# A streaming encoder step on one core: ScalarE's order written down, weights at fixed distances ahead, sums of squares in another bank, branch stages in half-range steps

## The chip, the cores and the metric

The kernel runs on one core of one Trainium2 chip. The metric is the device time of one launch in microseconds (us): 3112.74 us, the median of three runs (3103.7, 3112.74 and 3119.0). The engines are called as in the profile: PE (TensorE's matmuls; PEld is its weight loads), DVE (VectorE), ACT (ScalarE), POOL (GpSimd) and SP (SyncE, which issues most DMAs here).

## The reference, cut to what matters

One layer of a hybrid encoder over two requests that share weights: 2048 first frames of a new stream, and 64 frames of a running one. All data is fp32.

```
n = RMSNorm(h)
[z | xBC | dt | u | pool_gate | merge_logits] = n @ W_in            # 1024 x 10272
x, B, C = split(silu(causal_dwconv(xBC, 4 taps)))
per chunk of 64 frames, per group of 4 heads:                        # 8 groups
    L  = exp(acum[l] - acum[s]) for l >= s, else 0                   # acum = cumsum(dt * A)
    y  = (C B^T * L) @ (x dt) + (C @ state) * exp(acum)
    state = state * exp(acum[-1]) + B^T @ (x dt exp(acum[-1] - acum))
a = GatedGroupRMSNorm(y + D x, silu(z)) @ W_branch_ssd               # mean square over a group's 256 columns
b = (MultiScalePool(u) @ pool_w * silu(pool_gate)) @ W_branch_pool
h = h + (sigmoid(g_a) * a + sigmoid(g_b) * b) @ W_out;  y = RMSNorm(h)
```

Outputs are y of both requests and the carried states (SSD, convolution, pooling).

## The kernel before, in words

The 2112 frames are done in three parts of T = 704 frames, each in two halves of H = 352. Within a part, the columns of W_in come in pairs of 256 columns, and a `Pair` is computed by seven products instead of eight (a Strassen-like scheme, on sums of the blocks of W_in and on sums N[1..7] of the normalised input). Each weight block is split into a high and a low float32r piece (`split`: ACT writes the high one at L179, DVE the low one at L180), and each of the four k-steps takes three matmuls. So an *item* of PE's work is mostly one product of one pair: 12 matmuls of 352 columns.

`Stream` holds all items of all three parts in order, and *events* between them: functions that issue work of other engines, or a few matmuls, at a position counted in items. `prepare` fetches and splits weights for items ahead, as far as the eight weight slots are free. In `Pair.prep`, the step for product 1 loads both raw column blocks (`cols`, to a tile `wraw`), the step for product 6 has POOL compute three sums (L254 to L256), the step for product 5 a fourth (L260). The split blocks of the u, x and bc pairs are stored to memory in part 1 and loaded back in parts 2 and 3; z, gate and pool-gate pairs are split anew in each part. That makes 40 + 20 + 20 = 80 pairs with sums.

Within a product, results go through banks `a`, `d` and `e`; `keep` copies `a` to a tile e1, e2 or e3 on ACT (L282), and `store` (L290, L292) writes results out on ACT or adds them on DVE.

A part's phases are: u and pool-gate pairs; then for each of 8 groups its bc, x and z pairs, with the group's 6 SSD *units* (128 frames each, 48 units a part, 144 in all) placed in between as events; then gate pairs; then the pool branch, the SSD branch and the output product; and the norm of the next part.

A unit has four events. `unit_load` loads bA (the decay logarithms, L732, a DMA on ACT's queue) and POOL masks it (`affine_select`, L733). `unit_front` has ACT turn bA into exponentials (L749, four of them, one for each head) and PE transpose x and B (bank `tp`). `decay_load` loads eB. `unit_back` does PE's y product (bank `y`) and the new state's product (bank `st`); POOL scales the old state (L800), DVE reads y (L803, L804) and adds the new state to the scaled one (L805), which frees bank `st`.

After a group's last unit, `group_post` gates y; its square is taken on ACT (L817) and summed by two small matmuls with a column of ones (`group_rms`, tiles `sqr`, one call for each half, in bank `st`); in the last part `group_state` transposes both final states, one after the other, in bank `st`, and ACT copies each to a tile `ho` (L852).

PE runs its matmuls in program order (`mm` and `transpose` pin them). The order of ACT, DVE, POOL and of the DMA issues is chosen by the scheduler of the language, from what it assumes of durations, and is then fixed in the compiled program: each engine works through its list in order.

Of the kernel before, what the change touches and what calls it, by code (L numbers as in the profile page):

```python
# [8 lines left out]
F32 = mybir.dt.float32  # L9
# [7 lines left out]
P = 128  # L17
DM = 1024
KT = 8
# [47 lines left out]
class Stream:  # L67

    def __init__(self, slots):
        self.items, self.events = [], []
        self.slots, self.ready, self.out, self.n = slots, 0, 0, 0

    def add(self, prep, use, ns=1, free=None):
        self.items.append((ns, prep, use, [], ns if free is None else free))
        return len(self.items)
# [4 lines left out]
    def prepare(self, limit):  # L82
        while self.ready < len(self.items) and self.out + self.items[self.ready][0] <= limit:
            ns, prep, use, got, _ = self.items[self.ready]
            got.append(prep() if prep else None)
            self.out += ns
            self.ready += 1

    def run(self):
        ev = sorted(self.events, key=lambda e: e[:2])  # L90
        for i, (ns, prep, use, got, free) in enumerate(self.items):
            while ev and ev[0][0] <= i:
                ev.pop(0)[2]()
            self.prepare(self.slots)
            if use:
                use(got[0])
            self.out -= free
        for e in ev:
            e[2]()
# [3 lines left out]
def kernel(  # L103
# [24 lines left out]
    dma, dma_a = nc.sync.dma_start, nc.scalar.dma_start  # L128
    V, S, G = nc.vector, nc.scalar, nc.gpsimd
# [77 lines left out]
    def cunit(w, c0, r0=0):  # L207

        r = cols(w, c0, r0)
        out = []  # L210
        for i in range(2):
            s = split_slot(r[:, i * 512:(i + 1) * 512])
            out += [(s, k) for k in range(4)]
        return out
# [18 lines left out]
    class Pair:  # L233
# [6 lines left out]

        def prep(self, i):
            wd = wc_d.get(self.key)
            if wd is not None and not self.q.first:
                return load_slot(wd[:, i - 1])
            if i == 1:
                self.r0, self.r1 = [cols(w_in, c) for c in pair_cols[self.key]]
                self.a11, self.a12 = self.r0[:, 0:512], self.r0[:, 512:1024]
                self.a21, self.a22 = self.r1[:, 0:512], self.r1[:, 512:1024]
                src = self.a11
            elif i == 2:  # L250
                src = self.a12
            elif i == 6:
                self.s3 = s_tile()
                G.tensor_tensor(out=self.s3, in0=self.a11, in1=self.a21, op=ALU.subtract)  # L254
                G.tensor_tensor(out=self.a21, in0=self.a21, in1=self.a22, op=ALU.add)
                G.tensor_tensor(out=self.a11, in0=self.a21, in1=self.a11, op=ALU.subtract)  # L256
                src = self.a11
            elif i == 5:
                self.s4 = s_tile()
                G.tensor_tensor(out=self.s4, in0=self.a12, in1=self.a11, op=ALU.subtract)  # L260
                src = self.a21
            else:
                src = {7: lambda: self.s3, 4: lambda: self.a22, 3: lambda: self.s4}[i]()
            s = split_slot(src)
            if wd is not None:
                dma(wd[:, i - 1], flat_slot(s))
            return s
# [26 lines left out]
        def use(self, i, w):  # L294
# [26 lines left out]
            else:  # L321
                self.product(self.d, w, 3, False)
                self.store(self.d, 0, 1, self.e2)
                if self.tile_done:
                    self.tile_done(0)
                self.done()
# [22 lines left out]
    def row_scale(sp, ch, xt, junk):  # L349
# [5 lines left out]
        G.tensor_tensor(out=ss[0:L, 2:3], in0=ss[0:L, 1:2], in1=mhalf[0:L, 0:1], op=ALU.pow)  # L355
        S.activation(xt[0:L], xt[0:L], AF.Copy, scale=ss[0:L, 2:3])
# [64 lines left out]
    def begin():  # L421
# [9 lines left out]
        for ch in q.chunks:  # L431
# [4 lines left out]
            row_scale(n0, ch, xt, junk)  # L436
# [4 lines left out]
        stream.prepare(1)  # L441
# [10 lines left out]
        stream.prepare(2)  # L452
        s.factor(6)
        stream.prepare(3)
        s.factor(5)
        s.factor(7)
        stream.prepare(5)
# [21 lines left out]
        st.close()  # L479

    def add_part(qi, q):
# [39 lines left out]
        def dt_turn():  # L521
# [14 lines left out]
            V.scalar_tensor_tensor(out=ea, in0=dtf, scalar=-1.0, in1=dtf, op0=ALU.mult, op1=ALU.max)  # L536
            S.activation(ea, ea, AF.Exp, scale=-1.0)
# [10 lines left out]
            dtA = dts["A"] = tmp("dtA")  # L548
            V.tensor_tensor(out=dtA, in0=dt, in1=aneg.unsqueeze(1).broadcast_to([P, NC, 32]), op=ALU.mult)
            q.nacum, q.dtd, q.dec = stt("acum"), stt("dtd"), stt("dec")  # L550
            V.memset(q.dtd, 0.0)
            V.memset(q.nacum, 0.0)
# [36 lines left out]
        def u_pair(gi):  # L589
# [11 lines left out]
            def tile_done(jj):  # L601
# [19 lines left out]
                split(st["dhi"][:, jj], st["dlo"][:, jj], dd)  # L621
# [3 lines left out]
            return Pair(q, ("u", gi), open_, lambda: None, tile_done)  # L625

        def pg_pair(gi):
# [6 lines left out]
            return Pair(q, ("pg", gi), open_, lambda: S.activation(st["gs"], st["gs"], AF.Silu))  # L634

        def pool_prep(gi):
            praw = nm["pb"].tile([P, 512], F32, tag="praw", name="praw", bufs=1)
            dma(praw.rearrange("p (k c) -> p k c", c=256), pool_w[0, gi].rearrange("(k p) c -> p k c", p=P))
            return split_slot(praw)
# [29 lines left out]
        def conv_pair(g, name):  # L669
# [28 lines left out]
            return Pair(q, ("x" if name == "xx" else "bc", g), open_, done, tile_done)  # L698
# [491 lines left out]
```

## Time and profile before

| | |
|---|---|
| runs | 3103.7, 3112.74, 3119.0 us |
| profiled execution: its own time | 3116.79 us |
| its span | 3115.1 us |
| mean granted TensorE clock, of full speed | 0.972 |
| PE busy | 2903.4 us (93%), 18794 instructions |
| DVE busy | 1983.6 us (64%) |
| ACT busy | 1533.1 us (49%) |
| POOL busy | 849.0 us (27%) |

The span is cut into three parts of about 1000 us; the first has a start-up of some 50 us, and behind the last matmul stands a tail of 11 us. Stretches of the first part: u and pool-gate pairs until about 290 us, groups until 800, gate pairs until 850, branches and output until 1034; the second and third repeat this with stored weights. In the rows below a bracket behind an instruction says how long its engine had been idle before it, and what it waited for last.

### The profile page before, as it was taken

Reading aid. Unit: us, or ns where it says so; the run is one execution under the profiler, and the core shown is the slowest. Engines: PE = TensorE matmul, PEld = TensorE weight load, DVE = VectorE, ACT = ScalarE, POOL = GpSimd, SP = SyncE. Lnnn points to the kernel's source line nnn. Section 1 sums busy time; section 2 is a strip of 40 time slices with the busy share of each in tenths; the row PEclk is TensorE's granted clock in tenths of the full one; section 3 lists DMA queues with packets and bytes.
Section 4 is the critical chain, followed back from the end, with each engine's and each line's share of the span. In section 5 each row is a group of like instructions: output and inputs, shape, how many; then the busy total and the mean of one; then the engine's idle time right before and its main releaser. Section 6 shows DMA issues by size and latency. Waiting matters only on the chain. (4 is left out here: it accounts for less than half of the span.)

```text
span 3115.1 us, 50768 instructions
## 1 busy us (share of the span) xinstructions
PE 2903.4 (93%) x18794; PEld 2772.7 (89%) x18794; DVE 1983.6 (64%) x3444; ACT 1533.1 (49%) x2920; POOL 849.0 (27%) x996
## 2 busy tenths in 40 slices
PE   6989888989999999999999999999999999989998
PEld 6888888878899999989898899999999888879998
DVE  7767787887654566457667765365666666666532
ACT  5445566666443433356655653244355565555311
POOL 4344454445100022123323410012233233341000
PEclk8999999999999999999999999999999999999999
DMA  5565676774586664757576467465567756646743
GB/s 184 177 204 182 213 212 179 233 214 113 173 286 209 242 187 142 233 173 194 171 225 189 100 218 222 134 200 177 185 194 200 204 163 210 170 102 213 223 126 138
DMA packets 502796, 585.09 MB, mean 188 GB/s; under 512 B 43429, under 2 KB 400637, under 8 KB 502549
## 3 DMA queue, kind: packets, MB, share of 16 engines
q1 hardware_dynamic: 391189, 531.50, 52.9%
q10 hardware_dynamic: 111360, 50.36, 8.5%
q8 instruction: 148, 2.42, 0.3%
q14 instruction: 99, 0.81, 0.1%
HBM read 434.31 MB, written 147.44 MB: 187 GB/s over the span
## 5 line engine op out<-in xcount | busy, mean ns | idle before, releaser
L132 PE MATMUL ps_a<-N,w 128*128 128x352 f32 x5760 | 1022.0, 330 | 45.1 <-ACT e L282 42.3
L132 PEld LDWEIGHTS ps_a<-N,w 128*128 128x128 f32 x5760 | 946.6, 191 | 65.4 <-ACT e L282 51.3
L180 DVE TENSOR_TENSOR w<-wraw,w 128x512 fp32r<-128x512 f32 x560 | 462.6, 839 | 285.2 <-ACT w L179 276.7
L132 PE MATMUL ps_d<-N,w 128*128 128x352 f32 x2880 | 508.0, 332 | 4.3 <-DVE sa L292 3.0
L132 PEld LDWEIGHTS ps_d<-N,w 128*128 128x128 f32 x2880 | 477.5, 194 | 7.7 <-DVE sa L292 3.8
L179 ACT CAST w<-wraw 128x512 fp32r<-128x512 f32 x560 | 337.7, 618 | 253.8 <-POOL wraw L256 50.2
L749 ACT ACTIVATE bA<-bA,acum 128x128 f32<-128x128 f32 (+1 forms) x576 | 192.5, 385 | 259.0 <-POOL bA L733 250.4
L282 ACT COPY e<-ps_a 128x352 f32<-128x352 f32 x360 | 160.4, 446 | 303.4 <-PE ps_a L132 225.6
L132 PE MATMUL ps_e<-N,w 128*128 128x352 f32 x1440 | 265.1, 335 | 18.8 <-DVE zt L292 11.8
L132 PEld LDWEIGHTS ps_e<-N,w 128*128 128x128 f32 x1440 | 242.1, 196 | 22.6 <-DVE zt L292 13.0
L733 POOL TENSOR_SCALAR_AFFINE_SELECT bA<-bA 128x512 f32<-128x512 f32 x144 | 99.3, 689 | 426.7 <-DMA bA<-ac_d 404.3
L254 POOL TENSOR_TENSOR S<-wraw 128x512 f32<-128x512 f32 x80 | 125.0, 1563 | 214.9 <-DMA wraw<-in_w_in_dram 82.9
L689 DVE SCALAR_TENSOR_TENSOR xx<-raw,cwT,xx 128x704 f32<-128x704 f32 (+1 forms) x144 | 151.2, 1050 | 24.8 <-ACT xx L686 24.1
L800 POOL TENSOR_TENSOR h<-h,dec 128x256 f32<-128x256 f32 x136 | 101.6, 747 | 199.3 <-PE ps_y L132 196.9
L689 DVE SCALAR_TENSOR_TENSOR bc<-raw,cwT,bc 128x704 f32<-128x704 f32 (+1 forms) x144 | 139.3, 967 | 17.5 <-ACT bc L686 17.0
L260 POOL TENSOR_TENSOR S<-wraw 128x512 f32<-128x512 f32 x80 | 111.1, 1389 | 144.1 <-DVE w L180 132.4
L355 POOL TENSOR_TENSOR ss<-ss,mhalf 128x1 f32<-128x1 f32 (+1 forms) x18 | 11.0, 612 | 486.9 <-DVE ss L353 437.8
L132 PE MATMUL ps_a<-yn,w 128*128 128x352 f32 x798 | 131.3, 322 | 1.0 <-ACT w L179 0.8
L180 DVE TENSOR_TENSOR w<-S,w 128x512 fp32r<-128x512 f32 x160 | 114.5, 716 | 26.9 <-ACT w L179 26.9
L132 PE MATMUL ps_d<-yn,w 128*128 128x352 f32 x798 | 130.4, 322 | 0.0
L132 PEld LDWEIGHTS ps_a<-yn,w 128*128 128x128 f32 x798 | 128.0, 188 | 1.9 <-ACT w L179 1.1
L256 POOL TENSOR_TENSOR wraw<-wraw 128x512 f32<-128x512 f32 x80 | 117.5, 1468 | 41.6 <-DVE w L180 34.3
(292 smaller groups left out, 4976.2 us busy)
## 6 DMA issues: line engine op xcount, KB each, us to landing
wraw<-in_w_in_dram SPq DMA_DIRECT2D x160, 512.0 KB
w<-wc_x SPq DMA_DIRECT2D x112, 512.0 KB
w<-wc_bc SPq DMA_DIRECT2D x112, 512.0 KB
bA<-ac_d ACTq DMA_DIRECT2D x120, 256.0 KB
wc_x<-w SPq DMA_DIRECT2D x56, 512.0 KB
wc_bc<-w SPq DMA_DIRECT2D x56, 512.0 KB
w<-wc_u SPq DMA_DIRECT2D x56, 512.0 KB
wraw<-in_w_branch_ssd_dram SPq DMA_DIRECT2D x48, 512.0 KB
```

The lines of the kernel that those rows point to most:

```text
L132: tc.keep_in_program_order(nc.tensor.matmul(*a, **k))
L179: S.copy(out=dst_hi, in_=src)
L180: V.tensor_tensor(out=dst_lo, in0=src, in1=dst_hi.bitcast(F32), op=ALU.subtract)
L254: G.tensor_tensor(out=self.s3, in0=self.a11, in1=self.a21, op=ALU.subtract)
L256: G.tensor_tensor(out=self.a11, in0=self.a21, in1=self.a11, op=ALU.subtract)
L260: G.tensor_tensor(out=self.s4, in0=self.a12, in1=self.a11, op=ALU.subtract)
L282: S.copy(out=e, in_=ps[:, 0:H])
L355: G.tensor_tensor(out=ss[0:L, 2:3], in0=ss[0:L, 1:2], in1=mhalf[0:L, 0:1], op=ALU.pow)
L689: V.scalar_tensor_tensor(out=xx[:, i, 0:XL], in0=raw[:, t:t + XL], scalar=cwT[:, t, ct:ct + 1], in1=xx[:, i, 0:XL], op0=ALU.mult, op1=ALU.add)
L733: G.affine_select(out=bA[0:L, :, 0:L], in_=bA[0:L, :, 0:L], compare_op=ALU.is_ge, fill=-1e30, base=0, pattern=[[0, HPG], [1, L]], channel_ ...
L749: S.activation(bA[0:L, r, 0:L], bA[0:L, r, 0:L], AF.Exp, bias=q.nacum[0:L, ci, 4 * g + r:4 * g + r + 1])
L800: G.tensor_tensor(out=hd(hcur), in0=hd(hcur), in1=q.dec[:, ci, 4 * g:4 * g + 4].unsqueeze(2).broadcast_to([P, HPG, 64]), op=ALU.mult)
```

## The change

It has six pieces.

- **ACT's order is pinned.** From the end of `begin` on, copies, activations and DMA issues on ACT's queue are kept in the order of the program's text (class `S`, `dma_a`). So are POOL's weight sums (`pool_sum`) and its masks, the latter one item after bA's load was issued. DVE's order is still chosen by the scheduler.
- **Fixed distances.** An item's split is issued 5 items before its use and a stored block's load 7 before, where slots are free. The first raw load of a pair is issued 9 items before its product 1, the second 10 before product 6, three sums 7 before product 6, the fourth 12 before product 3. Some ACT work behind a product (Silu of z, x, bc and pool gate, splits of the pooled tile, softplus of dt) is issued some items later (`stream.later`).
- **Sums of squares in bank `y`.** `group_rms` moves from bank `st` to `y`, and stands behind the first `unit_front` that comes at least 4.4 items after `group_post`.
- **The final states** are transposed by two events, 1.5 items apart, and not behind each other.
- **Branch stages in half-range steps.** `pool_branch` and `ssd_branch` become two items each (one for each half of 352 frames, 24 or 48 matmuls), `out_product` one item for each block of 128 frames; gates, y and m0 are loaded and turned earlier, W_out's split happens in the pool branch's phase, and the next part's norm is spread over the output product, three items for each block of frames.
- **The last scaling** of an output block is done in 2 pieces of 512 columns instead of 4 of 256.

The work is nearly the same: PE has the same matmuls, ACT 147 table loads for 153.

PE's list at the end of the first group of part 1, before (bank `st` holds the new state of the group's last unit, the next unit's and then the squares' sum; `d`, `e` and `a` are products):

```order
L132 MATMUL ps_y_3313<-bA_3029,xdt_3116 64x128 x4
L132 MATMUL ps_y_3313<-bc_2850,h_3027 128x128 x2
L132 MATMUL ps_st_3320<-xdtd_3117,bt_3118 128x256
L132 MATMUL ps_d_3151<-N_149,w_3128 128x352 x12
L132 MATMUL ps_st_3347<-sqr_3206,onesr_111 32x352 x2
L132 MATMUL ps_d_3360<-N_151,w_3147 128x352 x12
```

and in the changed kernel:

```order
L183 MATMUL ps_y_3305<-bA_3022,xdt_3109 64x128 x4
L183 MATMUL ps_y_3305<-bc_2844,h_3020 128x128 x2
L183 MATMUL ps_st_3312<-xdtd_3110,bt_3111 128x256
L183 MATMUL ps_d_3143<-N_149,w_3157 128x352 x12
L183 MATMUL ps_d_3345<-N_151,w_3198 128x352 x12
L183 MATMUL ps_a_3204<-N_153,w_3219 128x352 x12
L186 MATMUL ps_tp_3385<-ident_81,xx_2624 128x128 x2
L186 MATMUL ps_tp_3385<-ident_81,bc_2844 128x128
L183 MATMUL ps_tp_3385<-bc_2844 128x128
L183 MATMUL ps_y_3399<-sqr_3279,onesr_111 32x352 x2
```

Between the matmul that writes a new state to `st` and the squares' sum stood one product; now three products and a unit's transposes stand there, and the sum is in bank `y`.

ACT's list at the first units of part 1, before (`e1` to `e3` are the copies that free bank `a`, `w` the high halves of weights, `bA` a unit's exponentials):

```order
L732 DMA bA_2406<-ac_d_126 128x4x128
L732 DMA bA_2486<-ac_d_126 128x4x128
L749 ACT_TABLE_LOAD
L749 ACTIVATE bA_2406<-bA_2406,acum_778 128x128
L179 CAST w_2051<-wraw_1951 128x512
L749 ACTIVATE bA_2406<-bA_2406,acum_778 128x128 x2
L179 CAST w_2068<-S_2009 128x512
L749 ACTIVATE bA_2406<-bA_2406,acum_778 128x128
L749 ACTIVATE bA_2486<-bA_2486,acum_778 128x128 x4
L282 COPY e3_2084<-ps_a_1957 128x352
```

and in the changed kernel:

```order
L177 DMA bA_2398<-ac_d_126 128x4x128
L170 CAST w_2400<-S_2296 128x512
L170 CAST w_2423<-wraw_2339 128x512
L170 COPY sa_2267<-ps_a_2235 128x11x32
L170 CAST w_2440<-wraw_2339 128x512
L170 COPY e2_2460<-ps_a_2380 128x352
L174 ACT_TABLE_LOAD
L174 ACTIVATE bA_2398<-bA_2398,acum_755 128x128 x4
L170 COPY bt_2473<-ps_tp_2466 128x128
L177 DMA bA_2478<-ac_d_126 128x4x128
```

The exponentials of two units, the second of them loaded just before, stood ahead of the copy `e3`; now a unit's exponentials stand together, behind the copies of the products before it, and the next unit's load is issued behind them.

The diff, cut to its core:

```diff
+    def later(self, k, fn):
+        self.pending.append((self.cur + k, fn))
+    def prepare(self, upto=None):
+        while self.ready < len(self.items):
+            ns, prep, use, got, free, lead = self.items[self.ready]
+            if self.ready - lead > self.cur or self.out + ns > self.slots:
+                return
...
+    class S:
+        @staticmethod
+        def pin(ins):
+            if fixed[0]:
+                tc.keep_in_program_order(ins)
+        @staticmethod
+        def copy(**k):
+            S.pin(nc.scalar.copy(**k))
...
+    def pool_sum(**k):
+        tc.keep_in_program_order(G.tensor_tensor(**k))
...
+            return {1: ((9, 1, self.load0),), 6: ((10, 1, self.load1), (7, 0, self.sums)),
+                    3: ((12, 0, self.sum4),)}.get(i, ())
...
-            if i == 1:
-                self.r0, self.r1 = [cols(w_in, c) for c in pair_cols[self.key]]
...
             dma_a(bA[0:L, :, 0:L], ac_d[4 * g:4 * g + 4, lt:lt + L].unsqueeze(0).broadcast_to([L, HPG, L]))
-            G.affine_select(out=bA[0:L, :, 0:L], in_=bA[0:L, :, 0:L], compare_op=ALU.is_ge, fill=-1e30, base=0,
+            stream.later(1, lambda: tc.keep_in_program_order(
+                G.affine_select(out=bA[0:L, :, 0:L], in_=bA[0:L, :, 0:L], compare_op=ALU.is_ge, fill=-1e30, base=0,
...
         def group_rms(g, h):
-            ps = tpsum("st")
+            ps = tpsum("y")
...
+            after[n, i] = stream.add(lambda pr=pr, i=i: pr.prep(i), lambda w, pr=pr, i=i: pr.use(i, w),
+                                     lead=7 if pr.stored() else 5, early=pr.early(i))
...
-                p = max(mid, ready("z", g)) + 0.01
+                p = max(mid, ready("z", g) + 1.5) + 0.01
+                after_f = [t for t in slots[u + 1:u + 1 + NC] if t >= p + 4.4] if g + 1 < NG else [p + 5, p + 8]
+                r0 = after_f[0]
+                r1 = [t for t in after_f if t >= r0 + 2][0]
                 stream.at(p, lambda g=g: group_post(g))
-                stream.at(p + 0.01, lambda g=g: group_sum(g, 0))
-                stream.at(p + 5, lambda g=g: group_rms(g, 0))
-                stream.at(p + 6, lambda g=g: group_state(g))
+                stream.at(p + 2, lambda g=g: group_square(g))
+                stream.at(p + 3.2, lambda g=g: group_sum(g, 0))
+                stream.at(r0 + 0.02, lambda g=g: group_rms(g, 0))
+                if q.last:
+                    stream.at(r0 + 0.03, lambda g=g: group_state(g, grp[g]["h"], ssd_p))
+                    stream.at(r0 + 1.5, lambda g=g: group_state(g, grp[g]["hs"], ssd_s))
...
-            stream.add(lambda j=j: cunit(w_bp, j * P), lambda u, j=j: pool_branch(j, u), 2)
+            stream.add(lambda j=j: column_blocks([got[0, j]]), lambda u, j=j: pool_branch(j, 0, u), 2, 0, 2,
+                       early=((4, 1, lambda j=j: get((0, j), w_bp, j * P)),))
+            stream.add(None, lambda u, j=j: pool_branch(j, 1, u), 0, 2)
```

## Rows read from the trace of the kernel before

**Rows 1.** Busy time by stretch: length, busy us (instructions) of each engine, clock.
```profile
core 0: us, PE busy (x) PEld busy (x) DVE busy (x) ACT busy (x) POOL busy (x), PEclk, DMA share, GB/s
50.00:290.00 240.00, 219.37 (x1328) 212.40 (x1329) 175.81 (x266) 110.26 (x203) 101.03 (x88) 0.96 0.61 200
290.00:800.00 510.00, 448.41 (x2883) 413.49 (x2882) 404.94 (x655) 320.08 (x612) 238.54 (x243) 0.95 0.62 184
850.00:1034.00 184.00, 183.25 (x1163) 181.87 (x1161) 93.86 (x148) 67.96 (x106) 1.01 (x2) 1.00 0.79 262
...
2300.00:2800.00 500.00, 463.32 (x3028) 431.27 (x3027) 334.27 (x627) 285.66 (x574) 172.24 (x253) 0.97 0.62 174
...
50.00:3104.00 3054.00, 2876.51 (x18670) 2749.60 (x18670) 1941.77 (x3351) 1500.35 (x2869) 830.90 (x972) 0.98 0.62 188
```

**Rows 2.** PE's waits, whole span: waiting for what: us, times, longest.
```profile
PE ps_st L132 <- DVE h L805: 50.7, 14, 8.4
PE ps_a L132 <- ACT e L282: 42.3, 27, 5.2
PE ps_st L135 <- ACT ho L852: 15.0, 8, 3.3
PE ps_e L132 <- DVE zt L292: 11.8, 3, 5.0
```

**Rows 3.** PE's waits in 290 to 800 us (the groups of part 1).
```profile
PE ps_st L132 <- DVE h L805: 34.0, 6, 8.4
PE ps_a L132 <- ACT e L282: 13.2, 11, 3.3
```

**Rows 4.** Timeline 405 to 428 us: start, duration, instruction, count, [idle before <- releaser].
```profile
417.43 1.29 POOL L254 TENSOR_TENSOR S<-wraw 128x512 f32<-128x512 f32 x1 [4.13 <-DMA wraw<-in_w_in_dram]
...
419.03 1.75 DVE L180 TENSOR_TENSOR w<-wraw,w 128x512 fp32r<-128x512 f32 x1
420.31 1.59 POOL L256 TENSOR_TENSOR wraw<-wraw 128x512 f32<-128x512 f32 x1
...
422.92 1.24 POOL L800 TENSOR_TENSOR h<-h,dec 128x256 f32<-128x256 f32 x1
...
424.83 0.41 DVE L804 TENSOR_TENSOR yt<-ps_y,yt 128x256 f32<-128x256 f32 x1
...
426.02 0.41 DVE L805 TENSOR_TENSOR h<-ps_st,h 128x256 f32<-128x256 f32 x1
...
426.58 0.77 PE L132 MATMUL ps_st<-sqr,onesr 128*32 128x352 f32 x2 [8.40 <-DVE h L805]
```

**Rows 5.** Timeline 219 to 231 us.
```profile
220.51 3.98 PE L132 MATMUL ps_d<-N,w 128*128 128x352 f32 x24
221.12 0.75 SPq L204 DMA_DIRECT2D wraw<-in_w_in_dram  x1
226.00 0.63 POOL L733 TENSOR_SCALAR_AFFINE_SELECT bA<-bA 128x512 f32<-128x512 f32 x1 [8.35 <-DMA bA<-ac_d]
226.67 1.28 ACT L749 ACTIVATE bA<-bA,acum 128x128 f32<-128x128 f32 x4 [7.89 <-POOL bA L733]
227.54 1.27 POOL L254 TENSOR_TENSOR S<-wraw 128x512 f32<-128x512 f32 x1 [0.90 <-DMA wraw<-in_w_in_dram]
...
229.21 0.43 ACT L282 COPY e<-ps_a 128x352 f32<-128x352 f32 x1
...
229.69 1.54 PE L132 MATMUL ps_a<-N,w 128*128 128x352 f32 x4 [5.20 <-ACT e L282]
```

**Rows 6.** Waits of all engines, whole span: us, times, longest.
```profile
POOL bA L733 <- DMA bA<-ac_d: 404.3, 97, 19.9
...
ACT bA L749 <- POOL bA L733: 250.4, 95, 8.3
```

**Rows 7.** DVE's groups by line, 850 to 1000 us: count, busy us, mean ns, idle.
```profile
L180 DVE TENSOR_TENSOR w<-wraw,w 128x512 fp32r<-128x512 f32 x51 | 33.4, 687 | 57.7 <-ACT w L179 57.5
```

**Rows 8.** The same in 300 to 800 us.
```profile
L180 DVE TENSOR_TENSOR w<-wraw,w 128x512 fp32r<-128x512 f32 x117 | 120.3, 1041 | 19.4 <-ACT w L179 19.2
```

More of the change, by code (lines that the diff above doesn't have):

```diff
@@ L87, in prepare, with first, soon @@
             self.ready += 1
-    def run(self):
[L90 to L94, printed above, removed]
+    def first(self):
+        self.pending = []
+        self.ev = sorted(self.events, key=lambda e: e[:2])
+        self.early.sort(key=lambda e: e[:3])
+    def soon(self, i):
+        while self.early and self.early[0][0] <= i:
+            self.early.pop(0)[3]()
+    def run(self):
+        for i, (ns, prep, use, got, free, lead) in enumerate(self.items):
+            self.cur = i
+            self.pending.sort(key=lambda e: e[0])
+            while self.pending and self.pending[0][0] <= i:
+                self.pending.pop(0)[1]()
+            while self.ev and self.ev[0][0] <= i:
+                self.ev.pop(0)[2]()
+            self.prepare()
+            self.soon(i)
             if use:
@@ L241, in prep @@
         def prep(self, i):
             wd = wc_d.get(self.key)
-            if wd is not None and not self.q.first:
+            if self.stored():
                 return load_slot(wd[:, i - 1])
-            if i == 1:
-                self.r0, self.r1 = [cols(w_in, c) for c in pair_cols[self.key]]
[L247 to L263, printed above, removed]
@@ L479, in begin @@
         st.close()
+        fixed[0] = True
     def add_part(qi, q):
@@ new lines, in y_load, with dense @@
+            ys.extend([(t, 0), (t, 1)])
+            return turn
+        def dense(ps, blocks, movs, off, ks, n):
+            for k in ks:
+                (s, c), (t, kk) = blocks[k], movs[k]
+                wh, wl = s[:, 0, c * P:(c + 1) * P], s[:, 1, c * P:(c + 1) * P]
+                a, b = t[:, 0, kk, off:off + H], t[:, 1, kk, off:off + H]
+                for i, (st_, mv) in enumerate(((wh, a), (wh, b), (wl, a))):
+                    mm(ps[:, 0:H], lhsT=st_, rhs=mv, start=k == 0 and i == 0, stop=k == n - 1 and i == 2)
@@ new lines, in add_part, with m0_load, ssd_branch, evict @@
+        m0s = {}
+        def m0_load(j):
+            m0s[j] = nm["py"].tile([P, T], F32, tag="rb", name="m0t", bufs=2)
+            dma(m0s[j], m0_d[j])
+        def ssd_branch(j, h, u):
+            u = held.setdefault(("s", j), u)
+            ga = gts[j]
+            def evict(ps, off):
+                V.tensor_tensor(out=ga[:, off:off + H], in0=ps[:, 0:H], in1=ga[:, off:off + H], op=ALU.mult)
+            if j == 0:
+                if h == 0:
+                    held["ps"] = [any_bank(), any_bank()]
+                    dense(held["ps"][0], u, ys, 0, range(14), 16)
+                else:
+                    dense(held["ps"][1], u, ys, H, range(14), 16)
+                    for i, off in enumerate((0, H)):
+                        dense(held["ps"][i], u, ys, off, range(14, 16), 16)
+                        evict(held["ps"][i], off)
+            else:
+                ps = any_bank()
+                dense(ps, u, ys, h * H, range(16), 16)
+                evict(ps, h * H)
+            if h:
+                V.tensor_tensor(out=ga, in0=ga, in1=m0s[j], op=ALU.add)
+                stream.later(1, lambda: split(nm["mhi"][:, j], nm["mlo"][:, j], ga))
@@ L1028, in add_part @@
         obase = len(stream.items)
         fin, hrow = [], {}
+        order = (NC - 1,) + tuple(range(NC - 1))
         def out_start():
+            close_pool("pt")
             close_pool("py")
```

417 lines of the change are left out of this document (244 added, 173 removed).

## The prediction

> **What bounds the kernel now.** I read the stretches first [rows 1]. From 50 to 3104 us PE is busy for 2876.51 of 3054 us; nothing else comes near that over the whole (DVE 1941.77, ACT 1500.35). Two quantities can be won while the matmuls stay the same: 3054 - 2876.5 = 177.5 us in which PE stands idle, and the clock. It was granted 0.98 of full speed on the mean, 0.02 x 3054 = 61 us lost. The reader is to see where: in 850 to 1034 us, the branches, PE is idle for 0.75 us and the clock is 1.00. Where PE is held up (290 to 800 us: 61.6 us idle; 2300 to 2800: 36.7) the clock is 0.95 and 0.97, which loses 25.5 and 15 us; 50 to 290 loses 9.6. Those three make 50 of the 61 us. So the loss of clock goes with the idle stretches, and I take it to shrink in proportion with them.
>
> Next, PE's waits [rows 2]: the first four are 50.7 us for a state addition ahead of the squares' sum, 42.3 for copies of bank a, 15.0 for the copy of a final state, 11.8 for an addition to z. They are spread thin behind that. The long ones are followed back in two pieces of the timeline.
>
> **The squares' sum.** In the worst case [rows 4] its matmul stood 8.40 us idle until 426.58. It needed bank st, which DVE's L805 freed at 426.43; that add waited for POOL's scaling of the state (422.92 to 424.16), and POOL had been held from 417.43 by weight sums whose raw block came late (4.13 us idle for the load). The change puts the sum in bank y and 36 matmuls and some transposes behind the state's matmul, where 12 were. Twelve matmuls are 1.99 us (24 in 3.98, [rows 5]), so 24 more give 4.0 us. In the groups of part 1 there are 6 waits of 5.7 us on the mean, 34.0 in all [rows 3]; 4.0 off each leaves 10. The other 8 have 16.7 us, 2.1 each, and go. Bank y is freed by L804, here 1.2 us before L805; DVE's list isn't pinned, so I count 0.3 us for each of the 6, 2 us. That is 50.7 - 10 + 2, about -42. The bounds: all of it, -50; or only one product more of room, at most 14 x 2.0 = 28 and less where a wait is shorter, -25. What is late next: POOL's chain is the same, so L805 stays late, and the next state product in st, a unit further on, is the next that could ask for it.
>
> **The copies of bank a.** The other case [rows 5]: POOL masks bA at 226.00, 8.35 us idle for its load; ACT's exponentials start at 226.67, 7.89 us idle for that; behind them on ACT stand copies, the one of bank a at 229.21, and PE has then been idle for 5.20 us. In the changed list the exponentials stand behind the copies of the products before, and a unit's load is issued a unit's time ahead, one unit's exponentials at a time. I take -30 of the 42.3 us: 27 waits, mean 1.6, of which those begun by a bA that was loaded too late go and those begun by late weight splits stay. The bounds are 0 and -42; a loss is priced among the rivals, since one mechanism makes it.
>
> **Final states.** 8 waits of 15.0 us, longest 3.3 [rows 2], come from two transposes behind each other in one bank. A product of 2.0 us now stands between: mean 1.9 each is covered, the longer leave some: -13, bounds 0 and -15.
>
> **The addition to z** is one of the many DVE additions queued behind others, 11.8 us in 3; the moved Silu and splits thin out what is in front of it. -4, bounds 0 and -12.
>
> **Branch stages, output, norm.** 0.75 us can be won in 850 to 1034. More and shorter items could lose something: weights of an SSD item are asked for two items (96 matmuls, 16 us) ahead, and a raw load took from 221.12 to 227.54, 6.4 us until its sum could start [rows 5]; with four splits of 0.69 us behind it [rows 7] that is 9.2 us, covered. Two pieces instead of four in the last scaling concern the tail of 11 us; the chain there is one evict, reduce and scale for each block as before: 0.
>
> **What pinning adds.** ACT's list now follows the text, so whatever waits at its head holds copies, splits and exponentials behind it, and PE waits for the copies. Some of this will happen. Below: nothing, if all heads are ready. Above: I take 25 us, half of the 50.7 of the largest wait that the scheduler's order makes; +10 lies between, nearer to nothing, since in the piece of ACT's list shown the head's work stands behind the copies that the products before need.
>
> **The sum**, for the profiled execution of 3116.8 us: -42 - 30 - 13 - 4 = -89 us of idle time, +10 new. Clock: 61 x 89 / 177.5 = -31 (bounds 0 and -61). In all -110, so 3007 us. The median of the runs, 3112.7, is 4.1 us below the profiled one: 3003, rounded to 3000.
>
> **A page's rule against the change.** DVE's low halves of raw blocks took 687 ns in 850 to 1000 us, where POOL is all but idle (1.01 us busy, [rows 1, 7]), and 1041 ns in 300 to 800 us [rows 1, 8]. One of them shows it: 1.75 us from 419.03, in the middle of the three sums that POOL did from 417.43 to 421.90 [rows 4]. The Trainium skill, "SBUF — State Buffer", section "Who interferes with whom", says that a DVE instruction with two inputs from SBUF and a GpSimd instruction that reads SBUF exclude each other, the later one waiting until the first has ended. The trace agrees in that the splits beside sums are the long ones. By that rule a sum put at a fixed distance meets DVE's splits just as often; it makes rival 1.
>
> **The rivals.**
> 1. DVE becomes the bound in part 1's groups. It is busy for 404.94 of 510 us there, 79% [rows 1], and 117 x (1041 - 687) ns = 41 us of that is the lengthening beside POOL [rows 7, 8], which stays. For it: if PE's stretch shrank by 48 us, DVE would be at 405 / 462 = 88%, with its work bunched. Against: elsewhere it is at 67% (334.27 of 500). If the stretch gives nothing, 24 + 2 (squares, of 34.0 less 10), 9 (copies, 13.2 x 30 / 42.3) and 13 of clock (25.5 / 61 x 31) are missing: -62, about 3050 us.
> 2. Slower: ACT's head is a unit's exponentials that wait for bA, in each of 144 units, and the copies behind them no longer pass. Mask waits for the load were 404.3 us in 97, up to 19.9; exponentials' waits 250.4 us in 95, 2.6 each [rows 6]. Without the copies' term the rest is -59 idle, -20 clock, +10: -69. From 69 / 144 = 0.48 us of lost PE time a unit it is no faster; at 1.0 us, less than half of ACT's mean wait, +75: 3190 us. Against: a unit's slot is several products, of 2.0 us each, and the copy that PE needs has another bank's product to hide behind.
> 3. No change: ACT's head is a split whose sum isn't done. In 80 pairs, the three sums begin two items (4 us) before the split of their last, and they run from 417.43 to 421.90, 4.5 us [rows 4]; so that split waits for some tenths of a us, and longer where the raw load is late, which is asked for 3 products (6 us) ahead of the sums and took 6.4 us [rows 5]. At 110 / 80 = 1.4 us a pair it eats the gain: 3110. Against: the split is 5 products, 10 us, ahead of its use.
> 4. Nearly everything goes: 30 us of idle time stay of 177.5, and 10 of 61 us of clock: -147 - 51 = -198, about 2915. For it: the waits are thin, and each has a cover that costs nothing; against: POOL and DVE are as busy as before.
>
> **Chances.** Forecast 0.48 (its own range 2950 to 3040), rival 1 0.17, rival 2 0.13, rival 3 0.09, rival 4 0.13. Runs of this kernel lie within 0.5% of each other, so 15 us either side count as the same. Faster: nearly all of the forecast and of rivals 1 and 4, 0.77; same: rival 3 and the edge of the first, 0.10; slower: rival 2, 0.13. The range, 2905 to 3105 us, takes in rivals 1 and 4 and half of rival 3, and leaves out rival 2 and some of what lies below.
>
> **What would show it.** Right: in PE's waits the squares' sum falls below 12 us, copies of bank a below 15, the final state's copy below 3; the clock in 290 to 800 us rises to 0.97 or more; PE's busy time falls by some 20 us through the clock alone; the branches stay within 2 us. Rival 1: DVE's share above 85% in part 1's groups, and PE waiting there for DVE's additions and splits under other names. Rival 2: ACT waiting for POOL's mask as before or longer, with PE's wait for bank a's copies above 80 us. Rival 3: ACT waiting for POOL's sums (L256's kind) for over 100 us, and PE for weights. The forecast is wrong as a whole if PE's idle time between 50 us and the last matmul doesn't fall below 120 us.

## The result, and the profile after

The changed kernel takes 3191.16 us (median of four runs, 3175.62 to 3198.72) where the kernel before takes 3108.22 us (four runs, 3102.16 to 3119.0): 1.0257 times as long, interval 1.0206 to 1.0307. It is slower; 3000 us had been forecast.

The profiled execution has a span of 3187.6 us, 72.5 more than before, at a mean clock of 0.970 (0.972 before). The first row stands beside the last of [rows 1]; then the groups and the pool branch of part 1, cut at the same places of PE's program:

```profile
50.00:3177.70 3127.70, 2894.78 (x18670) 2762.64 (x18670) 1935.72 (x3377) 1482.90 (x2891) 852.02 (x973) 0.97 0.59 184
266.00:788.40 522.40, 458.48 (x2966) 423.02 (x2965) 403.46 (x669) 323.44 (x631) 261.47 (x254) 0.96 0.63 189
835.00:931.70 96.70, 72.51 (x384) 68.69 (x384) 56.77 (x95) 36.87 (x63) 0.00 (x0) 0.88 0.92 307
```

The same two stretches of the kernel before, same columns:

```profile
270.90:793.80 522.90, 459.96 (x2966) 424.33 (x2965) 412.54 (x667) 325.69 (x625) 245.83 (x251) 0.95 0.62 184
832.80:899.90 67.10, 64.60 (x385) 62.43 (x385) 44.82 (x62) 31.06 (x41) 0.00 (x0) 0.97 0.85 272
```

PE's idle time between 50 us and the last matmul has risen from 177.5 to 3127.7 - 2894.8 = 232.9 us. The groups of part 1 take as long as before (those of parts 2 and 3 do not, as the table shows); the pool branch of part 1, with the same matmuls, takes 30 us longer. All phases, in us of the profiled executions, the three parts added (u: u and pool-gate pairs with the first pairs of group 0, until the first unit's y product; gates: from the last unit's y product to the pool branch; the last four columns belong to the experiments):

| phase | before | after | e1 | e7 | e9 | e14 |
|---|---|---|---|---|---|---|
| u | 677.4 | 657.9 | 678.4 | 679.3 | 650.0 | 652.1 |
| groups | 1495.6 | 1523.2 | 1457.8 | 1472.8 | 1432.1 | 1434.3 |
| gates | 117.0 | 143.3 | 129.3 | 141.4 | 143.9 | 117.9 |
| pool branch | 195.4 | 230.0 | 233.0 | 183.8 | 229.1 | 203.5 |
| SSD branch | 374.8 | 372.8 | 372.4 | 377.4 | 372.1 | 369.0 |
| output | 216.2 | 221.0 | 216.1 | 216.8 | 221.3 | 221.3 |
| span | 3115.1 | 3187.6 | 3125.9 | 3110.4 | 3087.6 | 3037.6 |

PE's waits in the changed kernel, against [rows 2] (what waits and for whom: us, times, longest):

```profile
PE ps_y L183 <- ACT zt L170: 48.2, 24, 5.5
PE ps_y L183 <- DVE yt L880: 34.2, 19, 4.1
PE ps_tp L186 <- DVE bA L839: 23.3, 19, 2.2
PE ps_a L183 <- ACT e L170: 22.5, 12, 5.1
PE ps_st L186 <- ACT ho L170: 14.0, 6, 3.5
PE ps_y L183 <- DVE sqr L231: 11.4, 12, 1.6
PE ps_d L183 <- ACT w L170: 10.6, 4, 6.0
```

The wait of 50.7 us for L805 is gone, and three stand in bank y, 93.8 us together, where one of 6.0 us (for L804) stood before. The sum waits for y's last reader (L880, 20.6 us in 12; the other 7 of these waits are a unit's own y product, as before) and for its own operand (sqr), and the next unit's y product for ACT's copy of the sum (zt). The transposes wait 23.3 us for DVE's reader of bank tp (8.6 before). The copies of bank a have fallen from 42.3 to 22.5 us.

Why that copy is late is seen in the timeline of the changed kernel in a group of part 2 (start, duration, instruction, [idle before <- releaser]):

```profile
1426.33 0.48 PE L183 MATMUL ps_y<-sqr,onesr 128*32 128x352 f32 x2
...
1430.83 0.51 DVE L353 TENSOR_TENSOR raw<-ps_d,e 128x352 f32<-128x352 f32 x1
...
1431.37 0.97 ACT L174 ACTIVATE xx<-raw,colT,cwT 128x704 f32<-128x704 f32 x1 [5.18 <-DVE raw L353]
...
1432.25 0.42 ACT L170 COPY zt<-ps_y 1x352 f32<-1x352 f32 x1
...
1432.73 0.66 PE L183 MATMUL ps_y<-bA,xdt 128*64 128x128 f32 x8 [2.10 <-ACT zt L170]
```

The sum was done at 1426.81 (1426.33 + 0.48). ACT stood idle for 5.18 us all the same: the first instruction of its list was the first step of a convolution, whose input DVE finished at 1431.34, and the copy stood behind it. In the gates of part 1 the head is a split of pooled tiles:

```profile
820.89 3.44 SPq L1023 DMA_DIRECT2D pgs<-p_d  x6
...
825.35 1.68 ACT L170 CAST pgs<-pgs 128x704 fp32r<-128x704 f32 x2 [8.23 <-DMA pgs<-p_d]
...
826.93 0.45 ACT L170 COPY e<-ps_a 128x352 f32<-128x352 f32 x1
...
827.43 3.52 PE L183 MATMUL ps_a<-N,w 128*128 128x352 f32 x12 [5.08 <-ACT e L170]
```

and in the pool branch of part 1 a sigmoid that waits for the load of a gate. SP's queue first:

```profile
850.46 0.32 SPq L1156 DMA_DIRECT2D wo_d<-w  x1
850.88 0.38 SPq L1147 DMA_DIRECT2D S<-in_w_out_dram  x1
851.32 1.19 SPq L1040 DMA_DIRECT2D gt<-g_d  x1
```

and then ACT's list, in the same stretch:

```profile
858.05 0.89 ACT L174 ACTIVATE gt<-gt,colT 128x704 f32<-128x704 f32 x1 [10.65 <-DMA gt<-g_d]
858.84 1.12 ACT L170 CAST w<-S 128x512 fp32r<-128x512 f32 x2
...
861.80 1.12 ACT L170 CAST w<-wraw 128x512 fp32r<-128x512 f32 x2
```

The gate's load leaves SP only behind a store and a load of W_out's split; ACT stands at the sigmoid for 10.65 us; the weight split behind it (861.80) ends what PE waited for at 862.46 (1.73 us; at 889.89 5.99 us). That this place of ACT's list makes the branch longer is refuted by e1 and e2 below.

### The profile page after: what moved, and what is told of

Same layout as the page of the kernel before. It is cut to its first block, busy times and chain, and to the rows that moved or that the text cites. A ratio compares the mean times of both kernels' runs of the same rounds, so it can differ in the third digit from the quotient of the medians.

```text
span 3187.6 us, 50453 instructions
## 1 busy us (share of the span) xinstructions
PE 2923.0 (92%) x18794; PEld 2787.5 (87%) x18794; DVE 1973.8 (62%) x3462; ACT 1513.5 (47%) x2938; POOL 876.0 (27%) x996
## 5 line engine op out<-in xcount | busy, mean ns | idle before, releaser
L183 PE MATMUL ps_a<-N,w 128*128 128x352 f32 x5760 | 1027.5, 332 | 25.5 <-ACT e L170 22.5
L231 DVE TENSOR_TENSOR w<-wraw,w 128x512 fp32r<-128x512 f32 x544 | 430.3, 808 | 122.6 <-ACT w L170 122.2
L170 ACT CAST w<-wraw 128x512 fp32r<-128x512 f32 x544 | 325.9, 616 | 130.7 <-POOL wraw L180 77.4
L180 POOL TENSOR_TENSOR S<-wraw 128x512 f32<-128x512 f32 x160 | 246.4, 1540 | 323.9 <-DVE w L231 207.6
L180 POOL TENSOR_TENSOR wraw<-wraw 128x512 f32<-128x512 f32 x160 | 247.2, 1545 | 87.1 <-DVE w L231 76.8
L174 ACT ACTIVATE bA<-bA,acum 128x128 f32<-128x128 f32 (+1 forms) x576 | 179.3, 382 | 116.8 <-POOL bA L808 116.0
L808 POOL TENSOR_SCALAR_AFFINE_SELECT bA<-bA 128x512 f32<-128x512 f32 x144 | 110.6, 768 | 342.4 <-DMA bA<-ac_d 315.8
L762 DVE SCALAR_TENSOR_TENSOR xx<-raw,cwT,xx 128x704 f32<-128x704 f32 (+1 forms) x144 | 165.4, 1148 | 33.3 <-ACT xx L174 33.1
L836 DVE TENSOR_TENSOR xdt<-ps_tp,dt 128x256 f32<-128x256 f32 x144 | 59.9, 416 | 195.6 <-ACT bt L170 195.4
L183 PE MATMUL ps_y<-bA,xdt 128*64 128x128 f32 (+1 forms) x1152 | 93.4, 284 | 61.8 <-ACT zt L170 48.2
L183 PEld LDWEIGHTS ps_y<-bA,xdt 128*64 128x64 f32 (+1 forms) x1152 | 60.1, 140 | 96.1 <-ACT zt L170 56.1
```

The lines of the kernel that those rows point to most:

```text
L170: S.pin(nc.scalar.copy(**k))
L174: S.pin(nc.scalar.activation(*a, **k))
L180: tc.keep_in_program_order(G.tensor_tensor(**k))
L183: tc.keep_in_program_order(nc.tensor.matmul(*a, **k))
L231: V.tensor_tensor(out=dst_lo, in0=src, in1=dst_hi.bitcast(F32), op=ALU.subtract)
L762: V.scalar_tensor_tensor(out=xx[:, i, 0:XL], in0=raw[:, t:t + XL], scalar=cwT[:, t, ct:ct + 1], in1=xx[:, i, 0:XL], op0=ALU.mult, op1=ALU.add)
```

## The experiments

Times are medians; the ratio is to the kernel before on the same chip, with its 95% interval. Phases come from one profiled execution of each. Executions of one kernel spread by up to 24 us, and the profiled ones of e1, e3 and e8 lie 6 to 11 us below their medians; so 10 to 15 us more or less in the groups are not read as an effect.

| run | edit, of the changed kernel if not said otherwise | us | ratio |
|---|---|---|---|
| e1 | ACT's order free | 3138.12 | 1.0064 (1.0039 to 1.0089) |
| e2 | free from the gates to the output | 3167.80 | 1.0167 (1.0148 to 1.0186) |
| e3 | W_out's split in the SSD branch | 3153.39 | 1.0112 (1.0087 to 1.0136) |
| e4 | squares' sum in bank st | 3191.03 | 1.0237 (1.0215 to 1.0259) |
| e5 | pinned in u phases only, and e3 | 3103.95 | 0.9971 (0.9952 to 0.9991) |
| e6 | POOL's order free | 3197.77 | 1.0273 (1.0240 to 1.0307) |
| e7 | the kernel before, with the sums moved | 3111.37 | 0.9982 (0.9967 to 0.9996) |
| e8 | sum's copy on DVE | 3171.02 | 1.0185 (1.0158 to 1.0211) |
| e9 | conv step and Silu one item later | 3093.40 | 0.9940 (0.9918 to 0.9961) |
| e10 | splits one item later | 3208.81 | 1.0309 (1.0289 to 1.0328) |
| e11 | e2, e3 and e8 | 3123.64 | 1.0033 (1.0019 to 1.0046) |
| e12 | e5 and e8 | 3127.91 | 1.0039 (1.0019 to 1.0059) |
| e13 | conv step alone one item later | 3149.08 | 1.0105 (1.0079 to 1.0131) |
| e14 | e2, e3 and e9 | 3039.72 | 0.9743 (0.9719 to 0.9767) |
| e15 | e1 and e9's edit | 3141.81 | 1.0076 (1.0054 to 1.0098) |
| e16 | e14, first tile's conv step later too | 3047.35 | 0.9776 (0.9752 to 0.9800) |

**e1 to e4: one cause each.** The edits:

```diff
-        fixed[0] = True                                              # e1
+        fixed[0] = None
...
+        stream.at(post_end - 0.01, lambda: fixed.__setitem__(0, False))   # e2
+        stream.at(obase, lambda: fixed.__setitem__(0, True))
...
-                stream.at(c1 + t, lambda n=n, i=i: out_keep(n, i))   # e3 (and the first two loads)
+                stream.at(c2 + t, lambda n=n, i=i: out_keep(n, i))
...
-            ps = tpsum("y")                                          # e4, in group_rms
+            ps = tpsum("st")
```

> The changed kernel with ScalarE's order left to the scheduler everywhere, as before the change; all else as changed. Theory A (the pinned list is the whole loss, wherever its head waits): gates (42.0, 40.6, 45.8 us in the three parts of the changed kernel, 35 before) return to about 35 each, the pool branch of part 1 (96.7 us, 67.1 before) to under 75, groups lose 10 to 20 us: about 3110 us. Theory B (the pool branch of part 1 is late because W_out's 16 loads were moved into it, and its list's head waits whoever orders it): gates return, -23, pool branch of part 1 stays above 90 us, groups (528, 505, 518) stay within 8 us each: about 3165 us.

> The changed kernel, ScalarE's order pinned in the pair and group phases, but left to the scheduler from the first load of pooled tiles (gates) to the first output product. Theory A: both the gates' 23 us and the pool branch's 30 us go: about 3135 us. Theory B: only the gates' 23 us go (the pooled tiles' splits no longer stand ahead of bank a's copies), the pool branch of part 1 stays above 90 us: about 3165 us.

> The changed kernel with the 16 loads, splits and stores of W_out moved from the pool branch of part 1 to its SSD branch; all else as changed. Theory A (order alone): the pool branch of part 1 stays at 90 us or more: 3190 us. Theory B (the loads crowd out gates' and weights' loads): it falls from 96.7 to about 68 us, the DMA share there from 0.92 to below 0.85, the SSD branch stays at 125 us: about 3162 us.

> The changed kernel with the sum of squares back in bank st, at its new late position; all else as changed. Theory C (moving the sum to bank y made the next unit's y product wait for ScalarE's copy of the sum, 48.2 us in 24, and the sum wait for DVE's reader of y, 34.2 us in 19): these two waits fall below 15 us together, groups of parts 2 and 3 fall by 10 to 20 us each, about 3145 us. Rival D (the room matters, not the bank: waits come back under the names of bank st): the sum of waits on banks y and st stays within 15 us, 3185 us.

e1: without the pins the groups fall by 65.4 us and the gates by 14.0, the u phases rise by 20.5, and the pool branch of part 1 stays at 98.3 us. (The expectations count the gates from some 5 us later than the table does.) The span is 61.7 us shorter, of the 72.5 that the change added (by the ratios to the kernel before, 1.9 of the 2.6%). Theory B is right that the pool branch is another matter, and A that the groups are the pins', though both gave them far too little; the 3138 us lie between the two expectations. e2: the gates return to 117.4 us, the pool branch of part 1 stays at 96.8, 3167.8 us, as B had it.

These two runs also settle what the sigmoid at the head of ACT's list costs in the pool branch. ACT's wait for gates' loads there, in the changed kernel (835 to 932 us):

```profile
ACT gt L174 <- DMA gt<-g_d: 38.0, 5, 10.6
```

and in e1 (821 to 919 us), with the row of the branch, columns of [rows 1]:

```profile
ACT gt L174 <- DMA gt<-g_d: 2.6, 3, 2.2
```

```profile
821.20:919.50 98.30, 70.94 (x385) 66.06 (x384) 59.63 (x97) 42.45 (x66) 0.00 (x0) 0.89 0.95 324
```

The wait goes (1.5 us in e2), and the branch is no shorter; so the pinned list's head is not the loss here. What the changed kernel, e1 and e2 have in common in this stretch is the traffic: some 30 MB at a DMA share of 0.92 to 0.96, where the kernel before moves 18 MB at 0.85.

e3: the pool branch of part 1 falls to 65.3 us; nearly the same stretch of that run, with the columns of [rows 1]:

```profile
825.00:890.00 65.00, 61.01 (x370) 58.72 (x368) 44.19 (x74) 29.09 (x47) 0.00 (x0) 1.00 0.81 268
```

The DMA share is 0.81 for 0.92, the clock 1.00 for 0.88, and the SSD branch, now with the split, takes 123.2 us (124.8). That settles that piece: it is the move of W_out's split, 31 us. Whether W_out's 512 KB stores and 256 KB loads fill the DMA engines or hold up SP's queue (its stores stood there for 33.1 us in 13 waits for DVE's half of the split), or the splits' own work tells, is not separated by these runs. The groups come out 12.8 us shorter in e3 too, although the edit touches nothing in them; that is within the scatter. e4: no difference (1527.4 us of groups); the waits are there under bank st's name, 88.3 us for the sum's copy, its operand and L881. Rival D holds: the bank is not what matters.

**e5 and e7: parts of the change by themselves.** e5 switches the pin on at a part's start and off 3.1 items before its first unit, and has e3's edit. e7 gives the kernel before the new positions (`after_f`, `r0`, `r1`) and bank y.

> The changed kernel with ScalarE's order pinned only in the u and pool-gate pairs of each part, left to the scheduler elsewhere, and with W_out's loads in the SSD branch. If the three pieces found so far add up (the order free: groups 1458 us instead of 1523, gates 129 instead of 143, output 216 instead of 221; pinned u and pool-gate phases 658 instead of 678; W_out late: pool branches 197 instead of 230), it takes 3117.9 of the profiled free kernel less 20 less 33: about 3075 us, below the kernel before by 1.4%. If the pieces depend on each other (ScalarE's slots in the SSD branch filled by W_out, DVE then late), 3095 us or more.

> The kernel before with one part of the change alone: the sums of squares in bank y, behind the first unit front at least 4.4 items after the group's post, orders all left to the scheduler. The prediction's first term: -42 us, and clock, with PE's wait for L805 in bank st gone from 50.7 to below 10 us: about 3060 us. Rival: the wait comes back as a wait on bank y (for DVE's reader or ScalarE's copy) and less than 15 us are won: 3100 us or more.

e5 misses the sum by 29 us, and its other expectation, 3095 us or more, holds (its 3117.9 us are the median of the kernel before; the free kernel's span is 3125.9, which makes the sum 3073). It has e1's groups nearly (1473.6), but the u phases gain 4 us only, not 20; why is open. e7 has PE's waits so:

```profile
PE ps_a L132 <- ACT e L282: 52.2, 27, 5.0
...
PE ps_y L132 <- ACT zt L834: 19.8, 11, 3.7
PE ps_y L132 <- DVE yt L804: 13.5, 11, 2.8
```

The groups fall by 22.8 us, half of the term forecast; 33 us stand in bank y, where 6.0 stood before. The gates rise by 24.4 and the pool branch falls by 11.6, so that the whole kernel gains 0.2%. In each part's gates PE now waits about 4 us for one of DVE's additions (11.5 us in 3; 3.0 before), with a granted clock of 0.89 to 0.93 there for 1.00. No pin is in this kernel: longer gates are not the pins' alone. The rival was nearer: 3111 us.

**e6 and e8: what does the list's head wait for?** e6 takes the pins from POOL's sums and masks; e8 has the copy `zt` done by DVE (`V.tensor_copy` for `S.copy`).

> The changed kernel with POOL's weight sums and masks left to the scheduler, ScalarE pinned. Theory E (POOL's pinned list, a mask waiting for its load ahead of weight sums, is what ScalarE's head waits for): groups fall from 1523 us by 25 or more, about 3160 us. Theory F (ScalarE's own list makes the loss, whatever its head waits for): groups stay within 12 us, 3180 to 3200 us.

> The changed kernel with the copy of the squares' sum out of bank y done by DVE, whose order is free, and not by ScalarE. If that one copy behind a waiting head is the groups' loss: PE's wait of 48.2 us in 24 falls below 15, groups from 1523 to about 1490 us, 3155 us. If the head holds whatever stands behind it: the wait is replaced by ones for copies of bank a and transposes of B, groups fall by less than 12 us, about 3185 us.

e6: groups 1519.8 us, theory F; POOL's pins cost nothing. e8: groups 1501.7 us, between its two expectations; the wait for `zt` is 23.8 us, on DVE now. The copy looks like one thing that the head holds back, not all; but it is not a sure gain: e11 and e12 below carry the same edit and lose.

**e9, e10, e13, e15: the head itself.** The edits of e9 (e13 has the first alone, e15 both on e1) and of e10:

```diff
-                    stream.later(1, lambda: self.tile_done(0))
+                    stream.later(2, lambda: self.tile_done(0))
...
-            return Pair(q, ("x" if name == "xx" else "bc", g), open_, (4, done), tile_done)
+            return Pair(q, ("x" if name == "xx" else "bc", g), open_, (5, done), tile_done)
...
-                                     lead=7 if pr.stored() else 5, early=pr.early(i))       # e10
+                                     lead=7 if pr.stored() else 4, early=pr.early(i))
```

> The changed kernel with the convolution's first step of a pair's last tile put one item later in ScalarE's pinned list (two items behind the product, and Silu five). In the groups of part 1 ScalarE stood at these steps for 52.7 us in 12 waits for DVE's additions. Theory G (the pinned list loses by work that stands at its head before its input is there): these waits halve and the groups fall from 1523 us by 10 or more: about 3175 us. Rival H (ScalarE's wait there is idle time nobody needs; the loss is elsewhere in the list): groups within 8 us, 3185 to 3195 us.

> The changed kernel with the splits of weights pinned 4 items ahead of their use instead of 5 (sums and loads where they were). In the groups of part 1 ScalarE stood at the heads of splits for 50.7 us (37.9 for sums, 12.8 for loads). Theory G: these waits fall to below 25, PE's waits for the sum's copy and for bank a's copies fall by 20 us over all, groups by 15 us: about 3165 us. Rival H: groups within 8 us, about 3190 us; and where splits get late, PE waits for weights (over 30 us) and it is 3200 us or more.

> The changed kernel with the convolution's first step of a pair's last tile one item later in ScalarE's pinned list, Silu left at four items. Theory G1 (that step, waiting for DVE's addition at the list's head, made the loss in the groups): groups near the 1432 us of the kernel that moved both, about 3095 us. Rival (Silu was the head that held): groups above 1500 us, about 3180 us.

> The changed kernel with ScalarE's order left to the scheduler everywhere, and the convolution's step and Silu one item later in the text. Theory G1 (only in a pinned list does the place hold others up): groups stay within 15 us of the free kernel's 1458 us, about 3138 us. Rival (the later step helps because DVE's additions or POOL's work get room): groups fall by 50 us or more, below 3100 us.

e9 takes 91 us off the groups and 98 off the median, far more than theory G had asked for. What ACT waited for, in the changed kernel:

```profile
ACT bA L174 <- POOL bA L808: 116.0, 51, 6.0
ACT xx L174 <- DVE raw L353: 109.3, 22, 7.7
ACT bc L174 <- DVE raw L353: 93.4, 24, 7.2
...
ACT w L170 <- POOL wraw L180: 77.4, 30, 8.7
...
ACT bc L174 <- DVE bc L762: 22.7, 15, 2.8
```

and in e9:

```profile
ACT w L170 <- POOL wraw L180: 144.7, 46, 6.9
...
ACT bA L174 <- POOL bA L808: 48.2, 35, 4.2
ACT bc L174 <- DVE raw L353: 40.7, 20, 4.3
ACT xx L174 <- DVE raw L353: 32.6, 17, 3.1
```

The waits at the convolution's steps fall from 202.7 to 73.3 us, that for masks by 68, and Silu's for DVE's taps (22.7 us for bc) falls below 13. The waits for weight sums grow by 67 us, and the kernel is faster all the same: that part of ACT's idle time held up nothing that PE needed. PE then waits in e9:

```profile
PE ps_a L183 <- ACT e L170: 22.9, 11, 5.6
PE ps_y L183 <- DVE yt L880: 19.2, 18, 3.1
PE ps_y L183 <- DVE sqr L231: 14.1, 12, 2.6
...
PE ps_y L183 <- ACT zt L170: 7.6, 3, 3.6
```

PE's waits for the sum's copy and y's reader fall from 82.4 to 26.8 us, those for DVE's reader of bank tp from 23.3 to 8.5.

e13: the step alone brings the groups to 1481.8 us, 41 of the 91; with Silu moved too, 50 more. Both expectations miss: each of the two moves gives about half. ACT's waits at the steps are down to 78.7 us in e13 already; those for masks, 108.5 us, fall only with Silu. Silu moved alone was not run. e10 goes the wrong way (3208.8 us; its groups, 1530.6 us, are within the scatter of the changed kernel's): its wait for sums hardly falls (77.4 to 73.0 us), that for masks grows to 146.3. So moving just any head later is not what helps. That PE is not held by what the splits wait for would explain it, and is not shown. e15: with ACT's order free, e9's edit changes nothing for the better (groups 1471.0 for 1457.8, 3141.8 us for 3138.1). The place of these steps costs only in a pinned list.

**e11, e12, e14, e16: together.**

> The changed kernel with three of its losses taken out and ScalarE still pinned in the pairs and groups: order free from the gates to the output product, W_out's loads in the SSD branch, the squares' sum copied by DVE. If they add up, as spans: 3187.6 - 26 - 33 - 22 = 3107 us, the kernel before within 0.5%. If they depend on each other: 3125 us or more.

> The changed kernel with ScalarE pinned only in the u and pool-gate pairs, W_out's loads in the SSD branch (3104 us so far), and in addition the squares' sum copied by DVE. There PE waits 27.4 us in 14 for ScalarE's copy of that sum. If DVE is earlier with it than ScalarE: about 3085 us, 0.9% below the kernel before. If DVE, busier, is as late: 3100 to 3110 us.

> The changed kernel with all that was found: the convolution's step and Silu one item later, W_out's loads in the SSD branch, order free from the gates to the output product. If the pieces add up: 3087.6 of span less 31 (pool branch of part 1) less 22 (gates) = 3035 us, 2.5% below the kernel before. If they depend on each other as in the run that took out three others: 3055 us.

> As the kernel with all that was found, and the convolution's step of the pair's first tile one item later too (so far at once behind the product). In the run with the last tile moved ScalarE still stood 73 us in 37 for DVE's additions ahead of these steps, and 145 us for weight sums. If that is still on PE's way: groups fall by 10 us or more, about 3025 us. If not: within 8 us of the kernel without it.

e11 misses its sum by 22 us of span (its second expectation, 3125 us or more, fits), e12 its first by 43 us of its median: with the copy on DVE, e11's groups are 1521.2 us (e2 and e3 alone had 1527.0 and 1510.4) and e12's 1502.2 (1473.6 without it). In e12 PE waits 33.2 us for DVE's copy, where it waited 27.4 for ACT's in e5; DVE is no earlier with it. Why is open, and these 6 us are the smaller part of the loss. e14 adds up to 2.6 us of its expectation (span 3037.6 for 3035) and is the fastest kernel, 2.57% under the kernel before:

```profile
50.00:3027.40 2977.40, 2856.95 (x18670) 2734.99 (x18670) 1960.01 (x3376) 1497.82 (x2891) 858.97 (x973) 0.99 0.62 193
```

PE's idle time is 120.5 us and the mean clock of its span 0.984. What is left of PE's waits:

```profile
PE ps_y L183 <- DVE yt L880: 24.5, 18, 2.6
PE ps_y L183 <- DVE sqr L231: 10.6, 11, 1.6
PE ps_a L183 <- ACT e L170: 10.2, 14, 2.4
```

e16: 3047.35 us, groups 1438.2: the first tile's step is not on PE's way.

## Why the prediction was wrong, point by point

The prediction's own sign that it is wrong as a whole came true: PE's idle time is 232.9 us, and not below 120.

**What pinning adds** is the step that failed. It was put at +10 us, at most 25, because in the piece of ACT's list shown the unit's exponentials stand behind the copies. I looked at the head that I knew from the trace of before, the masked bA, and not at the other work that the text now put in front: the convolution's first step, one item behind the product whose sum DVE has still to write, and its Silu. Measured by e1, the pins cost 61.7 us of span (groups +65.4, gates +14.0, output +4.9, u phases -20.5, rest -2); by the ratios to the kernel before it is 1.9 of 2.6%. Pinning as such isn't the loss: with two steps one item later (e9) the pinned groups are 25.7 us shorter than the free ones of e1.

**Branch stages, at nothing.** W_out's 16 loads, splits and stores went from the SSD branch, where DMAs and ACT had room, into the pool branch: +31 us (e3). The gates' loads stood behind them in SP's queue and ACT at the sigmoid, but with that wait gone the branch is as long (e1, e2); which of the traffic, SP's queue and the splits' own work makes the 31 us is open. I had asked whether the branches' own weights come in time, and not what is moved in among them.

**The squares' sum.** Forecast -42; e7 gives -22.8 us in the groups and 0.2% in all. The wait for L805 did go. What was missing is who comes next: y's reader, the sum's operand and the next user of the bank. The bank itself is indifferent (e4).

**The copies of bank a.** Forecast -30; 42.3 to 22.5 us, -20, in the changed kernel, -32 in e14. With ACT free they are 59.8 us (e1): here the pin does what the step said.

**Final states.** Forecast -13; 15.0 to 14.0. One product between the two did not hide ACT's copy; with ACT's order free 9.3 us are left (e1). **The addition to z.** Forecast -4; 11.8 to 5.2, right. **Clock.** Forecast -31, in proportion to 89 us less idle time. The idle time rose by 55.4 us instead, so the term came out with the other sign, and the step behind it holds: the same 18670 matmuls were busy for 2894.78 us where they had been for 2876.51, 18.3 more, and the proportion gives 61 x 55.4 / 177.5 = 19. In e14, with 57.0 us less idle time, they were busy for 19.6 us less, and the proportion gives 19.6. It is no law: e3, with 25 us more idle time, has 1.2 us more. Together, idle time (+55.4 for a forecast of -79) and clock (+18.3 for -31) make nearly all of the difference.

**The rivals.** Rival 2 gave 3190 us and 3191 came out, but that is luck: its signs are absent. ACT's wait for masks fell from 250.4 to 116.0 us, and PE's wait for bank a's copies did not pass 80. Its kind of mechanism, a head that holds the pinned list, is right; its place was wrong. Rival 1: DVE is busy for 403.46 of 522.4 us in the groups of part 1 (77%), no bound. Nor did the 41 us of lengthened splits stay, as it had assumed. In the groups of part 1 a low half of a raw block took 1039 ns before, and in the changed kernel:

```profile
L231 DVE TENSOR_TENSOR w<-wraw,w 128x512 fp32r<-128x512 f32 x123 | 103.6, 850 | 19.4 <-ACT w L170 19.2
```

In the pool and SSD branches, where POOL does nothing, it took 684 ns. So the lengthening is half of what it was; why is not shown. The rule that the Trainium skill gives ("SBUF — State Buffer", "Who interferes with whom"), that a DVE instruction with two inputs from SBUF contends with a POOL instruction that reads SBUF, agrees with these figures in direction: the splits are the longer ones where POOL works. Rival 3: ACT did stand at splits for sums, 77.4 us, but in e9 it stood there for 144.7 us and the kernel was 98 us faster. Rival 4, with 30 us of idle time left, is far off: the best kernel has 120.5.

## What to carry to other kernels

When an engine's order is written down, list for each instruction what it waits for and who stands behind it: not only at the stall that the old trace shows, but at all work that the new text puts in front of a copy that frees a bank. A step that reads another engine's result is to be set back by as much as the trace shows that engine to be late; here two steps moved by one item were worth 98 us, and the same edit nothing where the order was free. A long wait at the head of a list is no proof of a loss: ACT's waits for weight sums grew in e9 while the kernel got faster, and its waits for gates went in e1 while the branch stayed as long. Work that is moved into another phase is to be weighed against that phase's traffic and its queues.

## What the runs showed of the hardware that was not expected

With W_out's loads in it, the pool branch of part 1 ran at a DMA share of 0.92 and 307 GB/s; a gate's load then took from its issue at 851.32 to about 858.0 us, 6.7 us. PE stood idle for 24 us there. The granted clock was 0.88 of full speed on the mean, between its two levels (1.2 and 2.4 GHz), and 1.00 in the stretch without W_out's loads (e3). The same 384 matmuls kept PE busy for 72.5 us, for 64.6 before: idle time of 24 us came with 8 us of slower matmuls.
